# Moving sixteen tokens of the second block from one-hot matmuls to the DRAM gate table

## The chip, the cores and the metric

The kernel runs on one core of a Trainium2 chip. The metric is the device time of one execution in microseconds (us). TensorE is called PE here, VectorE DVE, ScalarE ACT, GpSimd POOL and SyncE SP, as in the profile. A name with a q (SPq, ACTq) is an engine's queue at work on a DMA issue.

## The reference

A two-layer decoder block on 256 tokens is followed by a second block that ends in a PEER layer, and the change touches only that layer. Each of 8 heads selects 16 of 128 x 128 experts for each token, and the gates are a softmax over the 16 scores:

```python
best, pos = lax.top_k(cand.reshape(T, PEER_HEADS, PEER_TOPK * PEER_TOPK), PEER_TOPK)
experts = jnp.take_along_axis(cand_idx..., pos, axis=-1)
gates = jax.nn.softmax(best, axis=-1).astype(h.dtype)
...
act = jax.nn.gelu(jnp.einsum('cd,ced->ce', xb, ub), approximate=False) * gb
return jnp.einsum('ce,ced->cd', act, vb)
```

## The kernel before

The kernel doesn't gather experts. It computes gelu(u_e . x) for all 16384 experts and 256 tokens, multiplies by a dense table of gates that is zero where an expert was not chosen, and multiplies the result by all v_e. `big` is [128 i, 128 j, 256 tokens] in SBUF.

The back part has four stages. In the **pq stage** p_q and p_s compute the scores. In the **u stage** (the loop over `c`, two keys each, 128 keys) PE runs 24 matmuls for a key (`proj_stat`, mm3 at L329 to L331). Between keys, `pump` hands out the routing of the tokens in pieces (`RU`): the top-16 searches on DVE, token block 0 first and block 1 after it. Every piece has a price in credits, and each key brings 1.3 credits. In the **hot stage**, the keys from HOT0 on in the same loop, block 1's gates are made by one-hot matmuls: `hot_make` builds one-hot tiles for four tokens on DVE, `hot_mm` runs four 128x128 matmuls on PE (L1581), and the result multiplies `big`. There is one such group of four tokens a key, 32 groups for 128 tokens. `gelu` treats the columns that already have gates apart, in the single buffer `gx`, and the product L1596 runs on DVE for up to 48 columns a key and on POOL above that. In the **v stage** `big` goes through `asplit` into the last product.

Block 0's 128 tokens take another way. Their gates are scattered into a zeroed table `gd` in DRAM by POOL's indirect DMAs with add (`scatter`, one for each head and rank, 128 in all, L1492, each preceded by a small memset). A head's DMAs are declared independent of each other; the next head's wait for them. The table is read back two keys at a time (`g_load`) and multiplied in on POOL (`g_mul`, L1539).

Weights come through `Stream`: SP loads 1 MB, ACT makes the rounded half `wh` (L231) and DVE the rest `wl` (L243). In the back part wh and wl have three buffers each, and the two halves of a key are written into the program two keys ahead of its matmuls, so wh of key n+3 may start when PE has finished key n.

Each engine works through its own instructions in program order, so one that waits holds up those behind it on that engine. A DMA issue is an instruction of the engine that issues it.

Of the kernel before, what the change touches and what calls it, by code (L numbers as in the profile page):

```python
# [9 lines left out]
F32 = mybir.dt.float32  # L10
I32 = mybir.dt.int32
# [4 lines left out]
OP = mybir.AluOpType  # L16
# [11 lines left out]
LAM_INIT = 0.8 - 0.6 * math.exp(-0.3 * 0)  # L28
NEG = -1.0e30
NE = 128  # L30
NZ = 32
CRED0, CRED1 = 2.0, 1.3
HOT0 = 91


def stat_pack(w):
# [227 lines left out]
def body(ctx, tc, I, O):  # L264
    nc = tc.nc
    V, A, P, G = nc.vector, nc.scalar, nc.tensor, nc.gpsimd
# [5 lines left out]
    dp = ctx.enter_context(tc.tile_pool(name="dp", bufs=1, space=bass.MemoryType.DRAM))  # L272
# [576 lines left out]
    lctx.close()  # L849

    fp2 = f2ctx.enter_context(tc.tile_pool(name="fp2", bufs=2))
    gd = dp.tile([128 * NE * 128, 1], F32, name="gd")
    gz = gd.rearrange("(a p f) o -> a p (f o)", a=NZ, p=128)
    zt = fp2.tile([128, 256], F32, name="zt", bufs=1)
    V.memset(zt, 0.0)
# [608 lines left out]

    spacer = bx.tile([1, 1], F32, name="spacer", bufs=1)

    BATCH = [(0, 1), (1, 3), (3, 5), (5, 8)]

    def weights(t, a, b):
        g, v = gate[:, t, a:b, :], best[:, t, a:b, :]  # L1470
        V.tensor_tensor(g, v, v[:, :, 0:1].to_broadcast([128, b - a, 16]), op=OP.subtract)
        A.activation(g, g, AF.Exp)

    def address(a, b):
        v = best[:, 0, a:b, :]
        V.scalar_tensor_tensor(v, ei[:, 0, a:b, :], float(NE), ej[:, 0, a:b, :], op0=OP.mult, op1=OP.add)
        V.tensor_scalar(v, v, 128.0, tok[:, 0:1], op0=OP.mult, op1=OP.add)
        V.tensor_copy(idx[:, a:b, :], v)

    def normal(t, a, b):  # L1480
        g = gate[:, t, a:b, :]
        su = bx.tile([128, 8], F32, name="gsu")[:, 0:b - a]
        V.tensor_reduce(su, g, axis=AX.X, op=OP.add)
        V.reciprocal(su, su)
        V.tensor_tensor(g, g, su[:, :, None].to_broadcast([128, b - a, 16]), op=OP.mult)

    sent = []

    def scatter(h):
        for k in range(16):  # L1490
            G.memset(spacer, 0.0)  # L1491
            d = G.indirect_dma_start(  # L1492
                out=gd, out_offset=bass.IndirectOffsetOnAxis(ap=idx[:, h, k:k + 1], axis=0),
                in_=gate[:, 0, h, k:k + 1], in_offset=None, compute_op=OP.add)
            for oh, o in sent:
                if oh == h:
                    tc.declare_no_dep(d.ins, o.ins, reason="other experts of one head")
            sent.append((h, d))

    def batch(a, b):  # L1500
        def first():
            weights(0, a, b)
            address(a, b)

        def second():
            normal(0, a, b)
            for h in range(a, b):
                scatter(h)

        return [(0.5, first), (0.4, second)]  # L1510

# [9 lines left out]
                    RU.extend(batch(a, b))  # L1521
    for i in range(8):
        RU.extend(route(i, 1))
    RU.extend([(0.5, lambda: weights(1, 0, 8)), (0.6, lambda: normal(1, 0, 8))])

    W.sub = [V, V]
    gv = gd.rearrange("(i j t) o -> i j (t o)", j=NE, t=128)
    GT = {}

    def g_load(c):  # L1530
        if c == 0:
            GT["t"] = bx.tile([128, 4, 2, 128], F32, name="oj", bufs=1)
        GT[c] = GT["t"][:, c % 4]
        nc.sync.dma_start(GT[c], gv[:, 2 * c:2 * c + 2, :])

    def g_mul(c):
        if c < NE // 2:
            b = big[:, 2 * c:2 * c + 2, 0:128]
            G.tensor_tensor(b, b, GT.pop(c), op=OP.mult)  # L1539

    for c in range(NE // 2):
# [46 lines left out]
    def gelu(c, ps):  # L1588
        n = 4 * HB[0]
        p3 = ps.rearrange("p (a b) -> p a b", a=2)  # L1590
        b = big[:, 2 * c:2 * c + 2, :]
        A.activation(b[:, :, :S - n], p3[:, :, :S - n], AF.Gelu)
        if n:
            x = bx.tile([128, 2, 128], F32, name="gx", bufs=1)
            A.activation(x[:, :, :n], p3[:, :, S - n:], AF.Gelu)
            late.append(lambda: (V if n <= 48 else G).tensor_tensor(b[:, :, S - n:], b[:, :, S - n:], x[:, :, :n], op=OP.mult))  # L1596

# [6 lines left out]
    for c in range(NC):  # L1604
        w = W.get(("u", c))
        ps = bank()
        if 2 * c + 2 >= NE - 32:
            assert not RU
        for k in range(2):
            e = 2 * c + k - HOT0  # L1610
            if 1 <= e < 33:
                hot_make(e - 1)
            w(k)
            while pend:
                pend.pop(0)()
            if c == NC - 1 and k == 1:
                g_mul(0)
                as0 = bx.tile([128, 4, 256], F32R, name="oi", bufs=1)
                AV += [(as0[:, 0, :], as0[:, 1, :]), (as0[:, 2, :], as0[:, 3, :])]
                asplit(0)  # L1620
                asplit(1)
            proj_stat(ps[:, k * 256:k * 256 + 256], w, k, xT)
            pump(CRED1)
            if e >= 0:
                assert not RU
            if e == 0:
                hot_T()
            gated()
            if 2 <= e < 34:
                hot_mm(e - 2, 2 * c)  # L1630
        pend.append(lambda c=c, ps=ps: gelu(c, ps))
    pend.pop(0)()
# [78 lines left out]
```

## Time and profile before

| what | value |
|---|---|
| time, median of 3 runs (lowest, highest) | 1691.44 us (1689.56, 1692.04) |
| the profiled execution | 1689.98 us, its span 1688.2 us |
| PE busy | 1644.9 us, 97% of the span |
| DVE, ACT, POOL busy | 1172.8, 814.9, 478.5 us (69%, 48%, 28%) |
| mean granted clock of PE | 0.993 |

A span is what the profile covers, and the 1.78 us between it and the execution's own time lie outside. Busy shares are means over stages, so the argument reads one stage at a time. A row of a timeline gives start, duration, engine, line, operation, tiles, and in square brackets how long the engine had been idle and whose event ended that.

### The profile page before, as it was taken

Reading aid. Unit: us, or ns where it says so; the run is one execution under the profiler, and the core shown is the slowest. Engines: PE = TensorE matmul, PEld = TensorE weight load, DVE = VectorE, ACT = ScalarE, POOL = GpSimd, SP = SyncE. Lnnn points to the kernel's source line nnn. Section 1 sums busy time; section 2 is a strip of 40 time slices with the busy share of each in tenths; the row PEclk is TensorE's granted clock in tenths of the full one; section 3 lists DMA queues with packets and bytes.
Section 4 is the critical chain, followed back from the end, with each engine's and each line's share of the span. In section 5 each row is a group of like instructions: output and inputs, shape, how many; then the busy total and the mean of one; then the engine's idle time right before and its main releaser. Section 6 shows DMA issues by size and latency. Waiting matters only on the chain.

```text
span 1688.2 us, 27583 instructions
## 1 busy us (share of the span) xinstructions
PE 1644.9 (97%) x11013; PEld 1499.3 (89%) x11013; DVE 1172.8 (69%) x2069; ACT 814.9 (48%) x1260; POOL 478.5 (28%) x446
## 2 busy tenths in 40 slices
PE   8899999999999998999999999999999999999997
PEld 6888999899999986897889999999999888888886
DVE  5897554666655465876557898899899666666665
ACT  5564444444444444564454555444433544444444
POOL 0542000110300012302025788878701211111111
PEclk9999999999999999999999999999999999999999
DMA  7436877455555545424445666766634666666665
GB/s 274 143 134 237 262 237 249 175 198 189 204 197 178 197 175 187 152 98 162 138 152 178 181 190 176 198 178 185 164 131 147 200 221 202 219 207 214 212 209 175
DMA packets 80417, 317.48 MB, mean 188 GB/s; under 512 B 25121, under 2 KB 41761, under 8 KB 45345
## 3 DMA queue, kind: packets, MB, share of 16 engines
q1 hardware_dynamic: 59120, 304.38, 52.5%
q0 software_dynamic: 20736, 10.56, 4.2%
q8 instruction: 86, 1.41, 0.3%
q10 hardware_dynamic: 432, 0.79, 0.1%
q14 instruction: 43, 0.34, 0.1%
HBM read 303.04 MB, written 10.55 MB: 186 GB/s over the span
## 4 chain that ended last, share of the span: by engine, by line
PE 55%; DVE 3%; issue 1%; DMA 1%; ACT 1%; POOL 1%; POOLq 0%; DVEq 0%; ACTq 0%; SPq 0%
PE mm L329 9%; PE mm L331 9%; PE mm L330 9%; PE acc L330 8%; PE acc L329 8%; PE acc L331 7%; PE acc L1581 2%; DMA xTl<-mTl 1%; DVE qkm L1062 1%; POOL wl L243 0%; PE mm L1460 0%; PE mm L1336 0%; PE mm L1303 0%; DVE wl L243 0%; DVE r L453 0%
## 5 line engine op out<-in xcount | busy, mean ns | idle before, releaser
L243 DVE TENSOR_TENSOR wl<-raw,wh 128x1024 fp32r<-128x1024 f32 (+1 forms) x511 | 630.8, 1253 | 259.4 <-ACT wh L231 257.6
L231 ACT ACTIVATE wh<-raw 128x1024 fp32r<-128x1024 f32 (+1 forms) x537 | 553.6, 1055 | 376.1 <-PE acc L331 186.8
L329 PE MATMUL mm<-xTh,wh 128*128 128x256 f32 x2328 | 659.3, 283 | 1.2 <-DVE mTl L378 1.1
L331 PE MATMUL mm<-xTh,wl 128*128 128x256 f32 x2328 | 654.9, 281 | 2.4 <-DVE wl L243 2.0
L330 PE MATMUL mm<-xTl,wh 128*128 128x256 f32 x2328 | 654.2, 281 | 0.0
L329 PEld LDWEIGHTS mm<-xTh,wh 128*128 128x128 f32 x2328 | 440.8, 189 | 4.0 <-DVE mTl L378 1.5
L331 PEld LDWEIGHTS mm<-xTh,wl 128*128 128x128 f32 x2328 | 440.4, 189 | 3.3 <-DVE wl L243 2.4
L330 PEld LDWEIGHTS mm<-xTl,wh 128*128 128x128 f32 x2328 | 440.8, 189 | 0.9
L1492 POOL DMA_INDIRECT gd<-slots,idx x128 | 253.0, 1977 | 68.9 <-issue 32.0
L330 PE MATMUL acc<-wl,xTh 128*128 128x512 f32 x632 | 251.7, 398 | 0.1
L329 PE MATMUL acc<-wh,xTh 128*128 128x512 f32 x632 | 250.6, 397 | 0.0
L243 POOL TENSOR_TENSOR wl<-raw,wh 128x1024 fp32r<-128x1024 f32 x26 | 64.7, 2494 | 565.1 <-ACT wh L231 563.3
L331 PE MATMUL acc<-wh,xTh 128*128 128x512 f32 x504 | 197.6, 392 | 0.0
L329 PEld LDWEIGHTS acc<-wh,xTh 128*128 128x128 f32 x632 | 119.1, 188 | 30.4 <-issue 0.7
L330 PEld LDWEIGHTS acc<-wl,xTh 128*128 128x128 f32 x632 | 119.0, 188 | 27.2 <-DVE wl L243 0.6
L1539 POOL TENSOR_TENSOR big<-big,oj 128x256 f32<-128x256 f32 x64 | 56.8, 888 | 289.8 <-DMA oj<-gd 289.8
L331 PEld LDWEIGHTS acc<-wh,xTh 128*128 128x128 f32 x504 | 94.6, 188 | 22.8
L880 DVE TENSOR_TENSOR sil<-sil,mm 128x256 f32<-128x256 f32 x44 | 18.5, 421 | 105.5 <-ACT sil L879 105.5
L879 ACT ACTIVATE sil<-mm 128x256 f32<-128x256 f32 x44 | 16.9, 385 | 151.2 <-PE mm L331 151.2
L362 DVE TENSOR_TENSOR xTh<-big,xTh 128x256 fp32r<-128x256 f32 x126 | 80.5, 639 | 0.0
L1491 POOL MEMSET spacer<- 1x1 f32 x128 | 78.6, 614 | 0.0
L330 PE MATMUL acc<-wl,hTh 128*128 128x512 f32 x176 | 69.6, 395 | 0.0
(388 smaller groups left out, 1838.4 us busy)
## 6 DMA issues: line engine op xcount, KB each, us to landing
raw<-in_ws_dram SPq DMA_DIRECT2D x131, 1024.0 KB
raw<-in_us_dram SPq DMA_DIRECT2D x64, 1024.0 KB
raw<-in_vs_dram SPq DMA_DIRECT2D x64, 1024.0 KB
gd<-zt SPq DMA_DIRECT2D x32, 256.0 KB
raw<-in_pq_dram SPq DMA_DIRECT2D x8, 1024.0 KB
oj<-gd SPq DMA_DIRECT2D x64, 128.0 KB
gb<-in_vec_dram POOLq DMA_DIRECT2D x12, 512.0 KB
gd<-slots,idx POOLq DMA_INDIRECT x128
```

The lines of the kernel that those rows point to most:

```text
L231: self.nc.scalar.activation(h[:, s], self.R[i][:, k * HW:(k + 1) * HW][:, s], AF.Copy)
L243: self.sub[k].tensor_tensor(l[:, s], self.R[i][:, k * HW:(k + 1) * HW][:, s], h.bitcast(F32)[:, s], op=OP.subtract)
L329: P.matmul(ps, lh, rh, start=first, stop=False)
L330: P.matmul(ps, lh, rl, start=False, stop=False)
L331: P.matmul(ps, ll, rh, start=False, stop=last)
L362: V.tensor_tensor(l, src, h.bitcast(F32), op=OP.subtract)
L879: A.activation(s, pg[:, :256], AF.Silu)
L880: V.tensor_tensor(s, s, pg[:, 256:], op=OP.mult)
L1491: G.memset(spacer, 0.0)
L1492: d = G.indirect_dma_start(out=gd, out_offset=bass.IndirectOffsetOnAxis(ap=idx[:, h, k:k + 1], axis=0), in_=gate[:, 0, h, k:k + 1], in_off ...
L1539: G.tensor_tensor(b, b, GT.pop(c), op=OP.mult)
L1581: P.matmul(ps[:, i * 128:i * 128 + 128], oi[:, i, :], oj[:, i, :], start=True, stop=True)
```

## The change

The table gets rows for 144 tokens instead of 128 (`TT`), so block 1's first sixteen tokens use it too, and the one-hot way keeps 112 (NG = 28 groups; HOT0 moves from key 91 to 95). A scatter wants 128 partitions: the sixteen tokens' 16 ranks are spread over them into `pack` by small DMAs on ACT's queue, eight strips of two ranks for the addresses and eight for the gates. A cast on DVE makes integer addresses `idx1` from `pack`, and each head then needs two scatters instead of sixteen. Block 1's softmax is cut into three batches of heads (0 to 1, 2 to 4, 5 to 7), each with its own strips and cast. The scatters of block 0's heads 5 to 7 now stand behind the first two of these batches, each together with a head of block 1.

```diff
-NZ = 32
+NZ = 36
+TT = 144
-HOT0 = 91
+HOT0 = 95
+NG = (2 * 128 - TT) // 4
...
-    gd = dp.tile([128 * NE * 128, 1], F32, name="gd")
+    gd = dp.tile([128 * NE * TT, 1], F32, name="gd")
...
+    pack = bx.tile([128, 2, 8, 2], F32, name="pack", bufs=1)
+    idx1 = bx.tile([128, 8, 2], I32, name="idx1", bufs=1)
+    groups = [((0, 5), (1, 0)), ((0, 6), (1, 1)), ((0, 7), (1, 2))] + [((1, h),) for h in range(3, 8)]
+    def batch1(a, b):
+        def first():
+            weights(1, a, b)
+            address(1, a, b)
+        def second():
+            normal(1, a, b)
+            for q in range(8):
+                for i, src in enumerate((best, gate)):
+                    A.dma_start(pack[16 * q:16 * q + 16, i, a:b, :], src[0:16, 1, a:b, 2 * q:2 * q + 2])
+            V.tensor_copy(idx1[:, a:b, :], pack[:, 0, a:b, :])
+            while groups and groups[0][-1][1] < b:
+                scatter(*groups.pop(0))
+        return [(0.7, first), (0.7, second)]
...
-            for h in range(a, b):
-                scatter(h)
+            for h in range(a, min(b, 5)):
+                scatter((0, h))
...
-    RU.extend([(0.5, lambda: weights(1, 0, 8)), (0.6, lambda: normal(1, 0, 8))])
+        for a, b in BATCH1:
+            if b == i + 1:
+                RU.extend(batch1(a, b))
...
-            GT["t"] = bx.tile([128, 4, 2, 128], F32, name="oj", bufs=1)
-        GT[c] = GT["t"][:, c % 4]
+            GT["t"] = bx.tile([128, 1024], F32, name="oj", bufs=1)
+        a = c % 3 * 2 * TT
...
-            if 1 <= e < 33:
+            if 1 <= e < NG + 1:
                 hot_make(e - 1)
```

On DVE, right behind the routing of block 1's second head (`big<-big,tf` and the sum into `slots` end it), the program before went on with the next head's search (MAX):

```order
L1428 TENSOR_TENSOR big<-cst,af 128x256
L1430 TENSOR_TENSOR big<-big,tf_11422 128x256
L1431 TENSOR_REDUCE slots<-big 128x16
L243 TENSOR_TENSOR wl<-raw,wh 128x1024
L1387 MAX tv_11592<-big 128x8
```

After the change the first batch of block 1 stands there:

```order
L1433 TENSOR_REDUCE slots<-big 128x16
L245 TENSOR_TENSOR wl<-raw,wh 128x1024
L1474 TENSOR_TENSOR slots<-slots 128x32
L1479 SCALAR_TENSOR_TENSOR slots<-slots 128x32
L1480 TENSOR_SCALAR slots<-slots,cst 128x32
L1487 TENSOR_REDUCE gsu<-slots 128x2
L1488 RECIPROCAL gsu<-gsu 128x2
L1489 TENSOR_TENSOR slots<-slots,gsu 128x32
L1518 CAST idx_8825<-pack 128x4
L245 TENSOR_TENSOR wl<-raw,wh 128x1024
```

Seven instructions moved between two wl, and the last of them, the cast (idx_8825 is `idx1`), reads what ACT's DMAs bring.

On ACT, at the same place of the program, before:

```order
L1592 ACTIVATE big<-mm 128x512
L231 ACTIVATE wh<-raw 128x1024 x2
L1592 ACTIVATE big<-mm 128x512
```

and now:

```order
L1619 ACTIVATE big<-mm 128x512
L1475 ACT_TABLE_LOAD
L1475 ACTIVATE slots<-slots 128x32
L1517 DMA pack<-slots 16x2x2 x16
L233 ACTIVATE wh<-raw 128x1024 x2
L1619 ACT_TABLE_LOAD
L1619 ACTIVATE big<-mm 128x512
```

Two table loads, one exponential and sixteen DMA issues stand between a gelu (L1592, now L1619) and the next wh. The batches of three heads look the same with 16x3x2; in the last one a wl stands behind the address (TENSOR_SCALAR) and a wh ahead of the DMAs.

On POOL, the last scatters ahead of the gelu products (now L1623), before:

```order
L1491 MEMSET spacer 1x1
L1492 DMA gd<-slots,idx 2097152x1
L1596 TENSOR_TENSOR big<-big,gx 128x2x52
L1596 TENSOR_TENSOR big<-big,gx 128x2x60
```

and now:

```order
L1496 MEMSET spacer 1x1
L1497 DMA gd<-pack,idx_8825 2359296x1
L1623 TENSOR_TENSOR big<-big,gx 128x2x52
L1623 TENSOR_TENSOR big<-big,gx 128x2x60
```

POOL's queue holds 144 scatters instead of 128 ahead of these products, and the last ten belong to five heads of block 1 with two each.

## Rows read from the trace of the kernel before

**Rows 1.** The page's busy time of each engine.

```profile
PE 1644.9 (97%) x11013; PEld 1499.3 (89%) x11013; DVE 1172.8 (69%) x2069; ACT 814.9 (48%) x1260; POOL 478.5 (28%) x446
```

**Rows 2.** Busy time by stretch: two windows of the u and v stages.

```profile
core 0: us, PE busy (x) PEld busy (x) DVE busy (x) ACT busy (x) POOL busy (x), PEclk, DMA share, GB/s
...
1100.00:1150.00 50.00, 50.00 (x423) 50.00 (x423) 44.96 (x118) 23.13 (x27) 39.82 (x40) 1.00 0.68 190
...
1340.00:1500.00 160.00, 160.00 (x688) 128.71 (x687) 101.88 (x116) 77.85 (x114) 24.88 (x29) 1.00 0.62 212
```

**Rows 3.** The chain that ended last, pq, u and hot stages: start, us, what.

```profile
927.02 1.84 PE mm L1460 x16
1190.89 0.33 PE mm L1563 x3
1196.91 0.89 PE acc L1581 x8
1200.62 0.89 PE acc L1581 x8
```

**Rows 4.** Timeline of ACT, u stage.

```profile
1076.88 1.06 ACT L231 ACTIVATE wh<-raw 128x1024 fp32r<-128x1024 f32 x1 [1.79 <-PE mm L330]
...
1079.73 1.06 ACT L231 ACTIVATE wh<-raw 128x1024 fp32r<-128x1024 f32 x1 [1.30 <-PE mm L330]
```

**Rows 5.** Timeline of DVE, the same place.

```profile
1077.98 1.22 DVE L243 TENSOR_TENSOR wl<-raw,wh 128x1024 fp32r<-128x1024 f32 x1 [0.38 <-ACT wh L231]
1079.12 0.29 DVE L1387 MAX8 tv<-big 128x8 f32<-128x128 f32 x1
```

**Rows 6.** Timeline of DVE: ends of a three-head batch of block 0.

```profile
1040.50 0.20 DVE L1471 TENSOR_TENSOR slots<-slots 128x48 f32<-128x48 f32 x1
...
1041.95 1.23 DVE L243 TENSOR_TENSOR wl<-raw,wh 128x1024 fp32r<-128x1024 f32 x1
```

**Rows 7.** Timeline of ACT: a table load, and a DMA issue with its successor.

```profile
1043.84 1.28 ACT L1592 ACT_TABLE_LOAD   x1
...
1682.48 0.37 ACTq L1685 DMA_DIRECT2D out_dram<-big  x1
1682.90 0.72 ACT L1682 ACTIVATE big<-big,rs 128x512 f32<-128x512 f32 x1 [0.45 <-POOL rs L320]
```

**Rows 8.** Timeline of SP: DMA issues that follow one another.

```profile
0.73 1.34 SPq L213 DMA_DIRECT2D raw<-in_ws_dram  x3
16.27 0.98 SPq L579 DMA_DIRECT2D cst<-in_cst_dram  x2
```

**Rows 9.** Timeline of POOL: first scatters of heads 0, 4, 5, 6, and the end.

```profile
908.81 2.38 POOL L1492 DMA_INDIRECT gd<-slots,idx  x1 [14.01 <-DVE slots L1485]
1071.05 1.56 POOL L1492 DMA_INDIRECT gd<-slots,idx  x1 [3.74 <-DMA gd<-slots,idx]
1110.88 1.56 POOL L1492 DMA_INDIRECT gd<-slots,idx  x1 [4.35 <-DVE big L1428]
1151.16 1.56 POOL L1492 DMA_INDIRECT gd<-slots,idx  x1 [2.13 <-DMA gd<-slots,idx]
1219.79 1.56 POOL L1492 DMA_INDIRECT gd<-slots,idx  x1 [0.27 <-issue]
1244.77 1.17 POOL L1596 TENSOR_TENSOR big<-big,gx 128x104 f32<-128x104 f32 x1 [23.42 <-ACT gx L1595]
```

**Rows 10.** Busy time by stretch: an idle time of PE and what followed.

```profile
659.00:664.00 5.00, 0.59 (x3) 0.34 (x2) 0.00 (x0) 0.99 (x3) 0.00 (x0) 0.79 0.98 402
664.00:669.00 5.00, 5.00 (x13) 3.90 (x13) 2.36 (x2) 3.88 (x5) 0.00 (x0) 0.53 0.15 30
```

**Rows 11.** PE's waits: us in total, times, longest.

```profile
PE mm L329 <- ACT vs L1002: 4.4, 1, 4.4
```

**Rows 12.** Timeline of POOL, v stage: one product with the table.

```profile
1359.55 0.97 POOL L1539 TENSOR_TENSOR big<-big,oj 128x256 f32<-128x256 f32 x1 [4.63 <-DMA oj<-gd]
```

**Rows 13.** Timeline of ACT, v stage: the split that reads it.

```profile
1361.37 0.40 ACT L361 ACTIVATE xTh<-big 128x256 fp32r<-128x256 f32 x1
```

More of the change, by code (lines that the diff above doesn't have):

```diff
@@ L1465, in body @@
     spacer = bx.tile([1, 1], F32, name="spacer", bufs=1)
+    BATCH1 = [(0, 2), (2, 5), (5, 8)]
     BATCH = [(0, 1), (1, 3), (3, 5), (5, 8)]
@@ L1472, in weights, with address @@
         A.activation(g, g, AF.Exp)
[L1474 to L1478, printed above, removed]
+    def address(t, a, b):
+        v = best[:, t, a:b, :]
+        V.scalar_tensor_tensor(v, ei[:, t, a:b, :], float(NE), ej[:, t, a:b, :], op0=OP.mult, op1=OP.add)
+        V.tensor_scalar(v, v, float(TT), tok[:, t:t + 1], op0=OP.mult, op1=OP.add)
+        if t == 0:
+            V.tensor_copy(idx[:, a:b, :], v)
     def normal(t, a, b):
@@ L1485, in normal, with scatter @@
         V.tensor_tensor(g, g, su[:, :, None].to_broadcast([128, b - a, 16]), op=OP.mult)
[L1487 to L1498, printed above, removed]
+    def scatter(*heads):
+        group = []
+        for t, h in heads:
+            ix, g = ((idx, gate[:, 0]), (idx1, pack[:, 1]))[t]
+            for k in range((16, 2)[t]):
+                G.memset(spacer, 0.0)
+                d = G.indirect_dma_start(
+                    out=gd, out_offset=bass.IndirectOffsetOnAxis(ap=ix[:, h, k:k + 1], axis=0),
+                    in_=g[:, h, k:k + 1], in_offset=None, compute_op=OP.add)
+                for o in group:
+                    tc.declare_no_dep(d.ins, o.ins, reason="other tokens, or other experts of one head")
+                group.append(d)
+    pack = bx.tile([128, 2, 8, 2], F32, name="pack", bufs=1)
[14 more added lines that the diff above has]
+        return [(0.7, first), (0.7, second)]
     def batch(a, b):
@@ L1502, in first @@
             weights(0, a, b)
-            address(a, b)
+            address(0, a, b)
         def second():
             normal(0, a, b)
-            for h in range(a, b):
-                scatter(h)
+            for h in range(a, min(b, 5)):
+                scatter((0, h))
         return [(0.5, first), (0.4, second)]
@@ L1523, in body @@
         RU.extend(route(i, 1))
-    RU.extend([(0.5, lambda: weights(1, 0, 8)), (0.6, lambda: normal(1, 0, 8))])
+        for a, b in BATCH1:
+            if b == i + 1:
+                RU.extend(batch1(a, b))
     W.sub = [V, V]
-    gv = gd.rearrange("(i j t) o -> i j (t o)", j=NE, t=128)
+    gv = gd.rearrange("(i j t) o -> i j (t o)", j=NE, t=TT)
     GT = {}
@@ L1531, in g_load @@
         if c == 0:
-            GT["t"] = bx.tile([128, 4, 2, 128], F32, name="oj", bufs=1)
-        GT[c] = GT["t"][:, c % 4]
+            GT["t"] = bx.tile([128, 1024], F32, name="oj", bufs=1)
+        a = c % 3 * 2 * TT
+        GT[c] = GT["t"][:, a:a + 2 * TT].rearrange("p (j t) -> p j t", j=2)
         nc.sync.dma_start(GT[c], gv[:, 2 * c:2 * c + 2, :])
@@ L1537, in g_mul @@
         if c < NE // 2:
-            b = big[:, 2 * c:2 * c + 2, 0:128]
+            b = big[:, 2 * c:2 * c + 2, 0:TT]
             G.tensor_tensor(b, b, GT.pop(c), op=OP.mult)
@@ L1593, in gelu @@
         if n:
-            x = bx.tile([128, 2, 128], F32, name="gx", bufs=1)
+            x = bx.tile([128, 2, 4 * NG], F32, name="gx", bufs=1)
             A.activation(x[:, :, :n], p3[:, :, S - n:], AF.Gelu)
@@ L1606, in body @@
         ps = bank()
-        if 2 * c + 2 >= NE - 32:
-            assert not RU
+        if 2 * c + 1 >= HOT0:
+            assert not RU and not groups
         for k in range(2):
             e = 2 * c + k - HOT0
-            if 1 <= e < 33:
+            if 1 <= e < NG + 1:
                 hot_make(e - 1)
@@ L1628, in body @@
             gated()
-            if 2 <= e < 34:
+            if 2 <= e < NG + 2:
                 hot_mm(e - 2, 2 * c)
```

## The prediction, made before the run

> **What bounds the kernel now.** I read the busy times first: PE is busy for 97% of the span [rows 1]. A mean hides stages, so the windows come next: in the u stage PE is busy for all of 50 us, in the v stage for all of 160 us, at granted clock 1.00 [rows 2]. DVE is the next engine, with 44.96 of 50 us. So in the stages that the change touches two things move the end: PE work that goes away, and any wait that PE doesn't have now. The chain of work that ended last gives PE's pace. From the end of the last p_s matmul (927.02 + 1.84 = 928.86) to the transposes of hot_T at 1190.89 there are 92 keys, 2.85 us each [rows 3]. In the hot stage the groups of one-hot matmuls follow each other at 3.71 us [rows 3], so a group costs PE 0.86 us.
>
> How much can PE's suppliers be late? Stream lets wh of a key start when PE has finished the key three before it. The wh that starts at 1076.88 was released by PE [rows 4]; counted from 928.86 at 2.85 us, 52 keys (0 to 51) had ended, so it belongs to key 54. PE comes to key 54 two keys later, at 1076.88 + 5.70 = 1082.6, and needs wl with its third matmul, 0.24 us on, at 1082.8. DVE has that wl done at 1077.98 + 1.22 = 1079.20 [rows 5]. The lead is 3.6 us, and three buffers allow no more: DVE had itself waited 0.38 us for wh [rows 5]. This is the number against which every new wait on DVE or ACT is held.
>
> **The change part by part.**
>
> *Removed.* Four groups of one-hot matmuls, 4 x 0.86 = 3.4 us of PE. PE is never idle in this stage, so all of it is on the path: -3.4 us. The four groups' work on DVE and ACT lies beside PE and gives nothing more.
>
> *Moved.* HOT0 is four keys later because the batches have more pieces in the queue of credits. The keys themselves cost the same.
>
> *The batches of block 1.* Before, block 1's softmax was one piece with no DMA. Now there are three batches, each a chain across DVE, ACT, the DMA queues and DVE again, and the cast that ends it stands in DVE's queue ahead of the next wl. Behind the cast wait wl, and behind wl PE. I follow the first batch, which stands behind wl of key 54 as counted above; T is the end of that wl, 1079.20.
>
> - The six small DVE instructions. Block 0's batch of three heads took 1041.95 - 1040.50 = 1.45 us with one cast more [rows 6]; I take 1.4. The exponential's table load of 1.28 us [rows 7] can run while ACT has nothing else, since ACT waits 1.3 to 1.8 us for PE at each key [rows 4].
> - The DMA issues. Addresses and gates alternate; the second DMA needs the gates, so from there ACT issues one after another, and the cast needs the fifteenth, the last of the addresses. Three issues on SP took 1.34 us and two took 0.98 [rows 8], 0.45 to 0.49 each from start to start. On ACT one takes 0.37 us, and the next activation starts behind it [rows 7]. I take 0.46, as back-to-back issues are the nearest row: 13 x 0.46 = 6.0 us to the start of the fifteenth, and 0.4 for itself. The ends are 0.37 and 0.49.
> - The landing. The nearest rows are also of scattered 4-byte elements: the first scatter of a head waits for the landing of the last one of the head before, 2.13 us at one place and 3.74 at another [rows 9]. I take 2.2, because nothing accumulates here, and keep 3.7 as the upper end.
> - The cast, 0.2 us, and the next wl, 1.2 us.
>
> Together 1.4 + 6.0 + 0.4 + 2.2 + 0.2 + 1.2 = 11.4 us from T. PE wants that wl one key after the one before, at T + 3.6 + 2.85 = T + 6.45. So PE waits 4.9 us. The second batch is the same, 4.9. In the third a wl stands behind the first three small instructions, which leaves 0.8 us less in the chain: 4.1. The sum is 13.9 us of PE waiting. Lower end: 13 x 0.37 + 0.4 + 2.1 + 2.8 = 10.1, so 3.7, 3.7 and 2.9, or 10.3. Upper end: 13 x 0.49 + 0.5 + 3.7 + 2.8 = 13.4, so 6.9, 6.9 and 6.1, or 19.9.
>
> The Trainium skill speaks against this order of work (DMA: Bandwidth & Descriptors, Rules for kernel authors): it advises to issue a DMA early, compute, and wait for its semaphore late. The cast waits at once. The same page (Issuing engines are not separate DMA queues) also says that the time in which a sequencer starts a DMA is usually small beside the DMA itself. Here the rows say the opposite, 6.4 us of issuing to 2.2 of landing; an estimate by that sentence, with no time for the issues, makes the chain 5 us, which the lead would cover.
>
> *What a stall does to PE's clock.* After an idle time of 4.4 us [rows 11] the granted clock was 0.79 over the 5 us that hold the wait and 0.53 over the next 5 [rows 10]. In these 5 us PE was busy throughout, and 0.47 of 5.0, 2.35 us, were lost. A wait of 4 to 5 us in the u stage is that long, but follows a full PE; no row shows such a one. Bounds are 0 and 2.35 each; I take 2.0, nearer to the row, and 6 us for three. The level would be the lower of the two, 1.2 GHz for a time.
>
> *POOL's scatters.* A head takes (1110.88 - 908.81) / 5 = 40.4 us with its wait [rows 9], 2.4 a scatter, so POOL is the pacer of the table and not routing. Heads 5 to 7 with two more scatters each take some 45 us apiece at that pace, and less late in the stage (heads 6 and 7 together took 70.2 us, from 1151.16 to 1221.35, against 80.8 at the mean pace): from 1110.88 to about 1241. Then five heads with two each, 3.9 us and a landing of 2.2: to about 1272. Before, the end was at 1221.4, and the first gelu product on POOL at 1244.77 [rows 9], 23 us of slack. That product comes four keys of 2.85 us later, at 1256, and with the three stalls (20 us with the clock) at 1276. So the stalls hide POOL's tail. Without them it would be late; that is a rival below.
>
> *Edits at nothing.* Four more zero fills of 256 KB lie in the first feed-forward stage, far ahead of their reader. The table's reads and products grow by an eighth: 0.97 us becomes 1.1, and ACT's split starts 0.85 us after the product's end (1361.37 against 1360.52) [rows 12, 13], which covers 0.1 for the product and 0.1 for the load; without that cover 64 x 0.2 us could at most be lost. Three slots for four in the table's buffer: each is free again when POOL's product has run, and a product takes a fifth of its 5.6 us. Four more table loads of 1.28 us on ACT lie inside ACT's idle time or the stalls.
>
> Sum: -3.4 + 13.9 + 6.0 = +16.5 us on the profiled execution's own 1689.98, or 1706.5. The median of the runs is 1.46 us above that execution, so I say 1707.
>
> **The rivals.**
>
> 1. *The stalls without the clock.* For it: the u stage keeps PE full up to the wait, and the row on the clock is from a stage with gaps. Time: 1689.98 + 10.5 = 1700.5.
> 2. *The lead covers the chain.* This is the other side: if issues are so quick that the chain stays under 6.45 us, no PE wait appears and the four groups are pure gain, 1689.98 - 3.4 = 1686.6. It decides at an issue spacing of (6.45 - 1.4 - 0.4 - 2.2 - 1.4) / 13 = 0.08 us. Against it stands every row of rows 7 and 8. It is also what would follow from the skill's sentence on small issue times.
> 3. *Covered, but POOL's tail comes late.* As 2, but POOL gets to its first gelu product at 1272 instead of 1256. The next gelu, 7.4 us after the first, can't write `gx`, ACT stands until 1273.4 instead of 1263.6, and wh and wl behind it come 9.8 us late against a lead of about 4: PE waits 6 us. -3.4 + 6 = +2.6, or 1692.6.
> 4. *Longer chains.* The small DMAs share the queues with 1 MB loads (DMA share 0.68 in the u stage [rows 2]) and with the scatters; at the upper end of issue and landing, with the clock's 7 us, +23.5, or 1713.5, and beyond if a DMA must wait for a load that is in flight.
>
> **How the numbers follow.** Forecast 0.50, rival 1 0.24, rival 4 0.12, rival 3 0.05, rival 2 0.06, and 0.03 that the parts cancel to nothing. Within 0.2%, 3.4 us, is about what a measurement of this kernel can't tell from no change. Faster gets rival 2, 0.06; same gets rival 3 and the cancelling, 0.08; slower the rest, 0.86. The range holds the forecast, rival 1 and most of rival 4, and takes in the bounds: the low end -3.4 + 10.3 = +6.9 gives 1697, and I start at 1696; the upper end 1713.5 plus the median's 1.5 gives 1715.
>
> **What would show it.** In the changed profile: three idle times of PE of 4 to 5 us near 1085, 1145 and 1210, ended by DVE's wl; DVE's cast waiting 7 to 8 us for a DMA on `pack`; sixteen ACT issues 0.46 us apart; PE's granted clock below 1 behind each wait; 28 groups at 3.71 us; POOL's scatters ending near 1272 with no wait of ACT for POOL behind it. The prediction is wrong if the cast finds its data there, if PE has no idle time in the u stage, or if the v stage has gaps from late table reads.

## The result, and the profile after

| kernel | median | ratio to before |
|---|---|---|
| before | 1690.86 us (1689.56 to 1692.04) | |
| after | 1715.85 us (1713.73 to 1717.52) | 1.0146 [1.0133, 1.0159] |

The change makes the kernel slower by 1.46%, 25 us, where the forecast was 16 us slower and its upper end 1715. The profiled execution of after took 1717.52 us, its span is 1715.7 us and its mean granted clock 0.986. The answer to [rows 1] is the page's busy time of each engine:

```profile
PE 1651.3 (96%) x10981; PEld 1504.7 (88%) x10981; DVE 1173.3 (68%) x2062; ACT 820.5 (48%) x1260; POOL 508.3 (30%) x476
```

The totals say almost nothing, and PE's busy time has even grown by 6.4 us although 32 matmul records are gone, eight for each of the four groups. The waits of PE between 1000 and 1330 us, that is in the u stage and the hot stage, say more. The columns are the total, the number of times and the longest; before, this list is empty for the same stretch.

```profile
engine line waited for: us in total, times, longest us
PE mm L331 <- ACT wh L233: 18.6, 3, 6.3
PE mm L333 <- DVE wl L245: 1.8, 3, 0.7
```

PE waits 20.4 us, and it is not DVE's wl but ACT's wh that ends 18.6 of them. The windows show the first idle stretch and what follows each of the three (the other two are 6.14 and 6.16 us long, at 1153.58 and 1222.75), and two rows that answer to [rows 2]:

```profile
core 0: us, PE busy (x) PEld busy (x) DVE busy (x) ACT busy (x) POOL busy (x), PEclk, DMA share, GB/s
1086.67:1092.94 6.27, 0.01 (x1) 0.01 (x1) 0.00 (x0) 1.12 (x2) 5.46 (x8) 0.70 0.25 1
1092.94:1099.45 6.51, 5.91 (x26) 5.62 (x27) 6.24 (x22) 3.71 (x4) 5.70 (x8) 0.50 0.62 163
1099.45:1106.00 6.55, 6.55 (x57) 6.55 (x57) 4.96 (x10) 3.29 (x4) 5.74 (x6) 1.00 0.66 163
...
1159.72:1164.30 4.58, 3.86 (x16) 3.56 (x17) 4.22 (x12) 3.71 (x4) 3.98 (x5) 0.50 0.65 125
...
1228.91:1235.98 7.07, 6.61 (x29) 6.32 (x30) 5.44 (x9) 5.53 (x7) 6.26 (x7) 0.50 0.41 85
1100.00:1150.00 50.00, 50.00 (x424) 50.00 (x423) 44.09 (x114) 23.97 (x28) 40.64 (x40) 1.00 0.70 190
1340.00:1500.00 160.00, 160.00 (x724) 130.44 (x723) 103.33 (x114) 79.19 (x118) 28.69 (x32) 1.00 0.62 212
```

In the idle stretch PE is busy for 0.01 us. When it resumes, the granted clock is 0.50, the lower level (1.2 GHz), for 6.5, 4.6 and 7.1 us, and then 1.00 again. PE is busy for 5.91 + 3.86 + 6.61 = 16.4 us at half clock; half of that, 8.2 us, is what these stretches cost. The lower clock alone is less: a matmul follows the next at 0.214 us there and at 2.85 / 24 = 0.119 later, which for the 71 matmuls (26 + 16 + 29) makes 6.7 us. Most of the rest lies in the first matmuls behind each wait, which start 0.38 us apart. Between the stalls, and in the v stage, PE is as full as it was in [rows 2].

ACT at the first stall shows what held wh (the line with x16 groups the sixteen regrouping DMAs of one batch):

```profile
1080.90 0.23 ACT L1475 ACTIVATE slots<-slots 128x32 f32<-128x32 f32 x1
1081.31 10.40 ACTq L1517 DMA_DIRECT2D pack<-slots  x16
1091.82 2.00 ACT L233 ACTIVATE wh<-raw 128x1024 fp32r<-128x1024 f32 x2 [10.69 <-DMA pack<-slots]
...
1100.61 1.06 ACT L233 ACTIVATE wh<-raw 128x1024 fp32r<-128x1024 f32 x1 [3.92 <-DMA raw<-in_us_dram]
```

And DVE at the same place; the answer to [rows 5] is its first line.

```profile
1079.14 1.22 DVE L245 TENSOR_TENSOR wl<-raw,wh 128x1024 fp32r<-128x1024 f32 x1 [0.38 <-ACT wh L233]
...
1081.59 0.19 DVE L1489 TENSOR_TENSOR slots<-slots,gsu 128x32 f32<-128x32 f32 x1
1092.94 0.17 DVE L1518 CAST idx<-pack 128x4 int32<-128x4 f32 x1 [11.16 <-DMA pack<-slots]
1093.04 1.23 DVE L245 TENSOR_TENSOR wl<-raw,wh 128x1024 fp32r<-128x1024 f32 x1
```

Both queues that feed PE stand still for over 10 us: ACT issues from 1081.31 to 1091.71, and wh follows; DVE waits 11.16 us with the cast, and wl follows. The releaser that the profile names in ACT's 10.69 is only the DMA that landed last; ACT waited for its own issues. The chain that ended last, at the same place, gives the price of each step (three of the issues that it goes through are shown, and one matmul at half clock):

```profile
1081.59 0.20 DVE slots L1489
...
1082.09 0.60 ACTq L1517
1082.72 0.61 ACTq L1517
...
1089.83 0.60 ACTq L1517
...
1090.47 2.39 DMA pack<-slots
...
1092.94 0.06 DVE idx L1518
...
1093.04 1.24 DVE wl L245
...
1094.90 0.21 PE mm L331
```

From the second issue to the fifteenth it is 1090.47 - 1082.09 = 8.38 us, 13 x 0.645. The fifteenth has landed 2.4 us after its start. Over all 48 the view of the tile `pack` has (duration in ns, lowest, median, highest):

```profile
L1517 ACTq DMA_DIRECT2D pack<-slots x48: 592/605/946, 1081.3 to 1227.1; - x48
```

The sum, by rows. The stage begins with the end of the last p_s matmul, 927.02 + 1.84 before [rows 3] and 928.17 + 1.85 = 930.02 after; from there to the end of the span it is 759.3 us before and 785.7 after, +26.4. Of these, -3.4 are the four groups, +18.6 + 1.8 the waits, +8.2 the half clock with the first matmuls behind the waits, and 0.9 the hot stage, where the 28 groups follow at (1339.39 - 1238.46) / 27 = 3.74 us in place of 3.71 [rows 3]. That makes 26.1. The 0.9 can't be put down to the change: run 2 below, with the same three stalls, and version 10 run the same 28 groups at 3.71, and the pace of the same instructions differs a little between executions (last section). The first and the last of these rows:

```profile
1238.46 0.89 PE acc L1608 x8
...
1339.39 0.89 PE acc L1608 x8
```

The remaining 1.15 us of the span lie ahead of the stage, where the change does nothing but zero fills; such shifts appear between all the kernels below (927.2 to 929.6 for the start of this row), so nothing is made of it. POOL's end answers to the last two of [rows 9]:

```profile
1268.70 1.60 POOL L1497 DMA_INDIRECT gd<-pack,idx  x1 [0.27 <-issue]
1286.67 1.17 POOL L1623 TENSOR_TENSOR big<-big,gx 128x104 f32<-128x104 f32 x1 [16.37 <-ACT gx L1622]
```

### The profile page after: what moved, and what is told of

Read it like the earlier page. It is cut to its first block, busy times and chain, and to the rows that moved or that the text cites. A ratio compares the mean times of both kernels' runs of the same rounds, so it can differ in the third digit from the quotient of the medians.

```text
span 1715.7 us, 27603 instructions
## 1 busy us (share of the span) xinstructions
PE 1651.3 (96%) x10981; PEld 1504.7 (88%) x10981; DVE 1173.3 (68%) x2062; ACT 820.5 (48%) x1260; POOL 508.3 (30%) x476
## 4 chain that ended last, share of the span: by engine, by line
PE 53%; DVE 3%; issue 2%; ACTq 2%; ACT 1%; DMA 1%; POOL 1%; POOLq 0%; DVEq 0%
PE mm L333 9%; PE mm L331 9%; PE mm L332 9%; PE acc L333 8%; PE acc L332 7%; PE acc L331 7%; ACTq L1517 2%; PE acc L1608 1%; DMA xTl<-mTl 1%; DVE wl L245 1%; DVE qkm L1064 1%; ACT wh L233 0%; POOL wl L245 0%; PE mm L1462 0%; PE mm L1338 0%
## 5 line engine op out<-in xcount | busy, mean ns | idle before, releaser
L331 PE MATMUL mm<-xTh,wh 128*128 128x256 f32 x2328 | 663.4, 285 | 19.7 <-ACT wh L233 18.6
L1566 POOL TENSOR_TENSOR big<-big,oj 128x288 f32<-128x288 f32 x64 | 59.6, 931 | 287.2 <-DMA oj<-gd 287.2
L1496 POOL MEMSET spacer<- 1x1 f32 x144 | 88.8, 617 | 0.0
L364 DVE TENSOR_TENSOR xTh<-big,xTh 128x256 fp32r<-128x256 f32 x126 | 85.5, 678 | 0.0
```

The costliest lines, as they stand in the source:

```text
L331: P.matmul(ps, lh, rh, start=first, stop=False)
L364: V.tensor_tensor(l, src, h.bitcast(F32), op=OP.subtract)
```

## The experiments

The theory after this reading (A): the loss is the sixteen DMA issues in ACT's queue, together with the cast that waits on DVE, three times over, and PE's lower clock behind each of the three waits. The rivals: only the cast and the landing hold PE (B), the larger table and the added scatters carry the loss (C), the clock costs nothing. Unless a diff says otherwise it is against after. Each ratio is to runs of before on the same chip.

**1. No regrouping DMAs.** Scatters of the sixteen tokens go to fixed cells that no token uses.

```diff
+    V.tensor_scalar(own, iota[:, 0:16], 1.0, 128.0, op0=OP.mult, op1=OP.add)
+    V.scalar_tensor_tensor(own, tok[:, 0:1].to_broadcast([128, 16]), float(NE * TT), own, op0=OP.mult, op1=OP.add)
+    V.tensor_copy(idx1.rearrange("p a b -> p (a b)"), own)
...
-            for q in range(8):
-                for i, src in enumerate((best, gate)):
-                    A.dma_start(pack[16 * q:16 * q + 16, i, a:b, :], src[0:16, 1, a:b, 2 * q:2 * q + 2])
-            V.tensor_copy(idx1[:, a:b, :], pack[:, 0, a:b, :])
```

> The 48 regrouping DMAs and the cast behind them are left out; the sixteen tokens' scatters go to fixed cells with a gate of zero, so their gates are left out of the result. Theory A (the loss is the sixteen DMA issues in ACT's queue and the cast that waits on DVE, three times, and PE's half clock after each): no PE idle time near 1087, 1154 and 1223, granted clock 1.00 there, the gain of four one-hot groups stays, 1687 to 1688 us; if POOL's scatters, which still end near 1269, are now late for the first gelu product on POOL, one PE wait of about 6 us near 1265 and 1692 to 1693. Rival C (the larger table, the ten more scatters or the longer table reads cost the time): still above 1705.

Measured: 1691.34 us, ratio 0.9994 [0.9985, 1.0004]. PE's only wait from 1000 us on is 0.4 us, and the clock stays at 1.00. All of the 25 us are gone with the 48 DMAs and the cast, so C falls. POOL's tail is there, as rival 3 of the prediction had it, first on POOL and then on ACT:

```profile
1270.98 0.99 POOL L1624 TENSOR_TENSOR big<-big,gx 128x104 f32<-128x104 f32 x1
```

```profile
1272.01 0.27 ACT L1623 ACTIVATE gx<-mm 128x120 f32<-128x120 f32 x1 [6.82 <-POOL big L1624]
...
1272.28 1.06 ACT L233 ACTIVATE wh<-raw 128x1024 fp32r<-128x1024 f32 x1
```

ACT stands 6.82 us for `gx`, but the wh behind it is only 4.9 us late (due about 3.7 us after the one of 1263.75, at 1267.4), and the lead takes all but 0.4 us of it. Rival 3's mechanism is real, its price was 0.4 us and not 6. In the profiled execution the stage's time (from the end of the last p_s matmul, 928.91 + 1.84, to 1687.1) is 756.4 us, 3.0 less than before: the four groups less this 0.4. The timed runs show less of it, -0.5 us at the median, with an interval from -2.5 to +0.7.

**2. Issues alone.** The fixed indices of 1, with the DMAs kept and only the cast gone, so DVE never waits for a DMA.

```diff
-            V.tensor_copy(idx1[:, a:b, :], pack[:, 0, a:b, :])
```

> The 48 DMAs are issued as they are, but the indices come from a fixed table and DVE's cast, which waited for them, is gone (the sixteen tokens' gates land in fixed cells). Theory A1 (ACT is blocked by its own issues: wh of the next key stands behind sixteen issues of 0.65 us): PE still idles three times, by about 5 us each instead of 6.2, since the landing and the cast drop out but wh and then wl must still follow the last issue; the clock still falls; 1709 to 1715 us. Rival B (what holds PE is only DVE's cast and the landing, as the prediction's chain has it, so that ACT's wh would have been in time): no PE idle time, 1687 to 1693 us.

Measured: 1715.47 us, ratio 1.0140 [1.0123, 1.0157], as slow as after. PE's waits:

```profile
PE mm L331 <- ACT wh L233: 18.6, 3, 6.2
PE mm L333 <- DVE wl L245: 1.4, 3, 0.5
```

ACT's own issues are enough to explain the whole loss, and B falls in the form in which it clears ACT. Waits of about 5 us were expected; that they are as long as in after says that the landing and the cast added nothing to them there.

**3. Issues on SP.** The other half: ACT is free, DVE's cast waits as in after.

```diff
-                    A.dma_start(pack[16 * q:16 * q + 16, i, a:b, :], src[0:16, 1, a:b, 2 * q:2 * q + 2])
+                    nc.sync.dma_start(pack[16 * q:16 * q + 16, i, a:b, :], src[0:16, 1, a:b, 2 * q:2 * q + 2])
```

> After's kernel with the 48 regrouping DMAs issued from SP instead of ACT; DVE's cast still waits for them at once. ACT's wh is then free. Theory A (ACT's queue and DVE's cast are each enough to hold PE): chain 1.4 + 14 x 0.645 + 0.6 + 1.7 + 0.2 + 1.2 = 14.1 us against 6.45, so three waits of 7 to 8 us ended by wl instead of wh, the clock falls as before, 1714 to 1722 us. Rival (ACT's blocked queue alone is the loss, and SP, whose issues of large loads are 0.33 to 0.49 us, is quick): waits under 4 us, 1703 us or less.

Measured: 1716.60 us, ratio 1.0154 [1.0139, 1.0170]. PE's waits, and one batch in SP's queue:

```profile
PE mm L333 <- DVE wl L245: 21.2, 3, 7.5
```

```profile
1077.68 0.33 SPq L217 DMA_DIRECT2D raw<-in_us_dram  x1
1081.49 10.30 SPq L1517 DMA_DIRECT2D pack<-slots  x16
```

Two more things could have held PE here, and didn't: SP's next 1 MB load starts only at 1094.03, but ACT's wh ran on time ahead of it (1081.18, 1083.93), and wl started at 1092.78, right behind the cast. On SP the sixteen issues take the same 10.3 us, so 0.64 us belongs to this DMA and not to ACT, and the 1 MB load beside it takes 0.33. The path that the prediction followed is also enough by itself. In after the two run side by side, and taking away either leaves the other.

**4. One pair for a batch.** The cast still waits, but for one pair of DMAs (the fixed indices of 1 serve for the other experts).

```diff
-            for q in range(8):
+            for q in range(1):
...
-            V.tensor_copy(idx1[:, a:b, :], pack[:, 0, a:b, :])
+            V.tensor_copy(idx1[0:16, a:b, :], pack[0:16, 0, a:b, :])
```

> One pair of DMAs for a batch instead of eight pairs, and the cast still waits for them (the sixteen tokens keep two of their sixteen experts; the others go to fixed cells with gate zero). Chain from the end of a wl: 1.5 small instructions + 1.3 for two issues + 2.0 landing + 0.2 cast + 1.2 wl = 6.2 us against a budget of 6.45. Theory A: no PE wait or less than 0.7 us each, the clock stays at 1.00, 1687 to 1694 us with POOL's tail as in the run without DMAs. Rival B (the landing and the waiting cast are the larger part): waits of 2 us or more remain, above 1698 us.

Measured: 1691.96 us, ratio 0.9998 [0.9986, 1.0009]; PE waits 0.5 us once. The first batch on DVE:

```profile
1084.58 0.19 DVE L1489 TENSOR_TENSOR slots<-slots,gsu 128x32 f32<-128x32 f32 x1
1086.50 0.16 DVE L1523 CAST idx<-pack 16x4 int32<-16x4 f32 x1 [1.73 <-DMA pack<-slots]
```

A landing that DVE waits for at once costs nothing as long as the chain stays inside the budget of 6.45 us. The number of issues is what breaks it. The four groups' gain doesn't show in the median. In the profiled execution (1692.77 us) the reason is PE's pace: a key took 2.88 us in place of 2.85 (last section), 3 us over the u stage. The other executions, from 1687.33 to 1695.30 us, left no trace.

**5. One batch of eight heads.** As many DMAs as one batch of after, with four times the bytes of its first.

```diff
-    BATCH1 = [(0, 2), (2, 5), (5, 8)]
+    BATCH1 = [(0, 8)]
-    groups = [((0, 5), (1, 0)), ((0, 6), (1, 1)), ((0, 7), (1, 2))] + [((1, h),) for h in range(3, 8)]
+    groups = [((1, h),) for h in range(8)]
...
-            for h in range(a, min(b, 5)):
+            for h in range(a, b):
```

> After's kernel with all eight heads of the sixteen tokens in one batch behind the last routing piece: sixteen DMAs once instead of three times, each of 16 partitions x 8 heads, and POOL's scatters of block 0 no longer paired. Theory A (each batch costs one wait of about 6.2 us plus about 3 us of half clock, independent of how many heads it carries): one PE idle time of 6 to 7 us near 1200 to 1210, one fall of the clock, 6.5 + 3 - 3.4 = +6 us on before, 1697 to 1699 us. Rival (the wait goes with the bytes, so a batch of eight heads waits as long as the three together): 18 us of idle time, 1710 us or more.

Measured: 1697.18 us, ratio 1.0039 [1.0027, 1.0051]. PE waits for wh once, 6.3 us, and twice for wl, 0.8 us together; an issue takes 0.61 us at the median, as in after. Four times the bytes cost the same: the price goes with the number of DMAs.

**6. PE kept busy.** Ahead of each of the three late keys (`FILL` counts three keys from the batch) PE gets matmuls that nobody reads, so that it doesn't idle.

```diff
+            while FILL and FILL[0] == 0:
+                FILL.pop(0)
+                zz = accp.tile([128, 512], F32, name="acc11")
+                for n in range(56):
+                    P.matmul(zz[:, 0:256], xT[0][:, n % KT, 0:128], xT[0][:, n % KT, :], start=True, stop=True)
             proj_stat(ps[:, k * 256:k * 256 + 256], w, k, xT)
```

> After's kernel with 56 matmuls of 128x256 whose result nobody reads, placed on PE just ahead of each of the three keys that wait, so that PE is busy for about 6.2 us of each wait. Theory D (about 9 of the 27 us are PE at its lower clock behind the three idle times): granted clock 1.00 throughout the u stage, the waits themselves stay filled, so 1706 to 1708 us, some 9 us less than after. Rival (the clock's fall costs nothing, the loss is all in waits): 1714 to 1718 us.

Measured: 1710.60 us, ratio 1.0114 [1.0098, 1.0131], 18.8 us above before where after is 25.0 above. The windows over the three places:

```profile
1085.00:1100.00 15.00, 13.76 (x111) 13.18 (x110) 7.95 (x23) 6.82 (x8) 12.88 (x15) 1.00 0.48 76
1150.00:1166.00 16.00, 15.07 (x125) 14.66 (x124) 8.69 (x25) 7.33 (x8) 13.85 (x17) 1.00 0.57 120
1218.00:1236.00 18.00, 17.58 (x149) 17.37 (x148) 10.98 (x22) 8.42 (x12) 12.62 (x16) 1.00 0.42 88
```

The clock stays at 1.00, and 6.2 us come back, not 9; the intervals of the two ratios leave this uncertain by some 3 us. The traces are sharper. By the starts of the keys, the four, two and three keys at the three places took 21.3, 14.7 and 19.7 us in after and 20.1, 13.8 and 17.1 here, 4.7 us less; the rest of the 7.3 us by which the stage is shorter in this profiled execution is PE's pace at the other keys (last section). The filling is dearer than the waits that it covers: 3 x 56 matmuls at 0.119 us are 20.0 us, and 2.5 us of waits remain, together 2.1 more than the 20.4 of after. So the full clock gives back 4.7 + 2.1 = 6.8 us, close to the 6.7 that the spacing of the matmuls said. The idle time is the cause of the lower clock.

**7. The table alone.** This one is an edit of the kernel before: the larger table, its fills and its slots, with no regrouping.

```diff
-NZ = 32
+NZ = 36
+TT = 144
...
-            GT["t"] = bx.tile([128, 4, 2, 128], F32, name="oj", bufs=1)
-        GT[c] = GT["t"][:, c % 4]
+            GT["t"] = bx.tile([128, 1024], F32, name="oj", bufs=1)
+        a = c % 3 * 2 * TT
+        GT[c] = GT["t"][:, a:a + 2 * TT].rearrange("p (j t) -> p j t", j=2)
```

> The kernel before with the larger table alone: 36 zero fills, cells of 144, three slots of 144 columns for the reads, and nothing of the regrouping (the products still take 128 columns, and all 32 one-hot groups stay). The prediction's edits at nothing: within 0.1% of before, 1689 to 1692 us, no PE wait in the last feed-forward stage. Rival (the table's longer reads, its slots or the fills carry part of the loss): 1.5 us or more above before.

Measured: 1690.44 us, ratio 1.0000 [0.9991, 1.0009], and no wait of PE from 1000 us on. The edits at nothing cost nothing.

**8. Strips in one run of bytes.** DVE turns the rows first; a DMA then carries addresses and gates together, in one contiguous run for each partition.

```diff
-            for q in range(8):
-                for i, src in enumerate((best, gate)):
-                    A.dma_start(pack[16 * q:16 * q + 16, i, a:b, :], src[0:16, 1, a:b, 2 * q:2 * q + 2])
+            for i, src in enumerate((best, gate)):
+                V.tensor_copy(turn[0:16, :, i, :, :], src[0:16, 1, a:b, :].rearrange("p h (q k) -> p q h k", q=8))
+            for q in range(8):
+                A.dma_start(pack[16 * q:16 * q + 16, 4 * a:4 * b], turn[0:16, q].rearrange("p i h k -> p (i h k)"))
```

> After's kernel, but DVE first turns the sixteen tokens' rows (two copies of some 0.2 us), so that a strip carries addresses and gates together and has one contiguous run of 32 or 48 bytes in each of its 16 partitions: eight DMAs for a batch instead of sixteen, SBUF to SBUF and on ACT as before, and the cast waits at once. What makes an issue of 0.60 us, where the regrouping through DRAM took 0.33? View E (the strided form of a strip with its three dimensions): issues fall to about 0.33, 0.37 apart; chain 1.4 + 0.5 + 7 x 0.37 + 2.0 + 0.2 + 1.2 = 7.9 us against 6.45, PE waits 1.5 us three times, 1691 to 1696 us. View F (SBUF to SBUF over 16 partitions, whatever the form): issues stay at 0.6, 0.645 apart; chain 9.8 us, PE waits 3.4 us three times and the clock falls in part, 1699 to 1708 us.

Measured: 1699.12 us, ratio 1.0044 [1.0028, 1.0059]. The issues, and PE's waits:

```profile
L1525 ACTq DMA_DIRECT2D pack<-gx x24: 514/611/905, 1081.0 to 1211.8; - x24
```

```profile
PE mm L331 <- ACT wh L233: 5.2, 3, 1.8
PE mm L333 <- DVE wl L245: 3.0, 3, 1.2
```

View F: the form of the strip is not what makes an issue 0.6 us. With half as many issues the waits are 8.2 us in place of 20.4, and the clock still falls three times.

**9. Through DRAM, and late.** Two DMAs for a batch in place of sixteen: one writes the turned rows to DRAM in the target's order, one reads them back to 128 partitions. They stand in pieces of their own between the routing pieces of the next head, the cast and the scatters in a third one.

```diff
+            for i, src in enumerate((best, gate)):
+                V.tensor_copy(turn[0:16, :, i, :, :], src[0:16, 1, a:b, :].rearrange("p h (q k) -> p q h k", q=8))
+            A.dma_start(hop[:, :, 4 * a:4 * b].rearrange("q p x -> p q x"), turn[0:16].rearrange("p q i h k -> p q (i h k)"))
+
+        def third():
+            A.dma_start(pack[:, 4 * a:4 * b], hop.rearrange("q p x -> (q p) x")[:, 4 * a:4 * b])
+
+        def fourth():
+            V.tensor_copy(idx1[:, a:b, :], mine[:, 0])
...
-HOT0 = 95
+HOT0 = 97
...
-(V if n <= 48 else G)
+(V if n <= 64 else G)
```

> A version that should beat both: DVE turns the sixteen tokens' rows to the order of the target (two small copies), one DMA writes them to DRAM and one reads them back to 128 partitions a key or more later, and the cast and the scatters come later still, so ACT issues 2 DMAs for a batch instead of 16 and nothing waits at once. hot_T two keys later, and the products of the first 16 groups on DVE so that POOL's tail is hidden. Theory A: no PE wait near 1087, 1154 and 1223, clock 1.00, the four groups are gained: 3.4 us under before, 1686 to 1689 us. Rival (the detour through DRAM or the reads behind it hold ACT or DVE again): waits of PE of 2 us or more in these places, 1692 us or more.

Measured: 1689.48 us, ratio 0.9988 [0.9979, 0.9997], and one wait of PE, at another place:

```profile
PE acc L331 <- ACT oi L363: 1.5, 1, 1.5
```

It stands ahead of the first v matmul. The table's first read can't start before the last one-hot group has left the buffer, and the groups now end with the last but one key.

**10. The same, one key earlier.** `HOT0 = 96`, nothing else.

> The version with the regrouping through DRAM, and hot_T one key earlier than there (one key later than in after), because its only PE wait of 1.5 us, ahead of the first matmul of the v stage, came from the table's first read behind the last one-hot group. Theory A: no PE wait from 1000 us on, 3 to 3.5 us under before, ratio 0.998. Rival (the wait stays, another read holds it): as that version, 1.5 to 2 us under before.

Measured: 1685.41 us, ratio 0.9966 [0.9955, 0.9978]. No wait of PE from 1000 us on. Its two kinds of DMAs and the cast, with the first and the last start:

```profile
L1528 ACTq DMA_DIRECT2D pack<-hop x3: 326/326/345, 1083.9 to 1203.3; - x3
L1531 DVE CAST idx<-pack x3: 163/163/217, 1097.5 to 1206.0; 128x6 int32<-128x6 f32 x2, 128x4 int32<-128x4 f32 x1
...
L1525 ACTq DMA_DIRECT2D hop<-gx x3: 325/326/334, 1082.1 to 1199.3; - x3
```

This version beats both kernels. In the profiled execution the stage takes 1685.8 - (928.23 + 1.84) = 755.7 us, 3.6 less than before: the four groups, by their working 3.4. The timed runs gain 5.8 us at this ratio.

**11 and 12. Where the rest of the gain is not.** Version 10 with the products' limit back at 48, and the kernel before with that limit at 64.

```diff
-(V if n <= 64 else G)
+(V if n <= 48 else G)
```

> The version through DRAM with hot_T at key 96, but the products of the late columns go to POOL after 12 groups again, as in after, instead of 16. It asks whether POOL's tail costs anything, and whether that version's gain of 6 us, where four groups are worth 3.4, holds on another chip. POOL's scatters end near 1270, ACT waits 5 to 7 us for gx once, PE at most 0.5 us. Expected 0 to 0.5 us above that version, ratio to before 0.997 to 0.998. Rival (the shift of two products to DVE is worth 2 us or more): ratio 0.998 to 0.9995 here, and a gain in the kernel before with the same shift.

> The kernel before with that one edit: the products of the late columns go to POOL after 16 groups instead of 12. PE waits for nothing there in before, so nothing should change: ratio 0.999 to 1.001, 1690 to 1692 us. Rival (it carries part of the 6 us gained): 2 us or more under before.

Measured: 1685.61 us, 0.9965 [0.9952, 0.9977], and 1691.96 us, 1.0001 [0.9992, 1.0010]. The gain holds on another chip, and the limit has no part in it. POOL's scatters again end at 1271.4 us, but the wait of ACT for `gx` that was expected isn't there: with hot_T a key later the next gelu, at 1272.08, finds POOL's product ended at 1271.85. In the profiled execution the stage is 3.5 us shorter than before. That the timed runs gain some 2 us beyond the four groups stays unexplained: no stage of the profiled executions shows it. PE's pace, which differs between executions (last section), could be part of it; that was not tested, as the other executions left no trace.

## Why the prediction was wrong

- **What bounds the kernel, and the budget.** Right. wl of key 54 ends at 1080.36, and PE would have taken up the next one at 1086.74, 6.4 us later (6.45 predicted). Run 4 shows that a chain inside this budget is free, runs 2 and 3 that one beyond it is not.
- **The step that failed: the issues, "I take 0.46".** One issue took 0.605 us and followed at 0.645; thirteen of them were 8.4 us and not 6.0. The chain from the end of that wl was 13.9 us (1080.36 to 1094.28) in place of 11.4, and all of the difference is in this term and in 0.3 us more for the first issue. The rows chosen [rows 7, 8] were of DMAs between DRAM and SBUF with 0.37 to 0.49 us, and the upper end, 0.49, came from them too. The trace of before had dearer ones, which the prediction passed over: SP's 32 zero fills of the table, 0.52 us at the median and 1.18 for two (rows below this list). By the prediction's own reckoning that is 0.59 an issue, 13 x 0.59 = 7.7 us against the 8.4 measured. An SBUF-to-SBUF strip on ACT or SP had no row there. Waits of 7.5 us for that wl follow, where 4.9 were said: 6.3 ended by wh, 0.6 by wl, and the matmuls between them at half clock.
- **The path that was left out.** The prediction let only the cast hold PE. wh of the next key stands in ACT's queue behind all sixteen issues, and run 2 shows that this alone makes the full loss. With 0.46 us an issue it would have been late too (16 x 0.46 + 1.06 for wh), so the omission hardly changed the sum, but a remedy on DVE alone would have brought nothing.
- **The landing.** 2.4 us from the issue's start to the release, against 0.4 + 2.2. Right.
- **The third batch.** Its shorter chain was not shorter in effect: ACT's issues began at 1215.25 for the addresses and went on when the gates were there, behind one more wl, and PE waited 6.2 us for wh.
- **The clock.** The mechanism is right. Read as the prediction read its row, half of PE's busy time at 0.50, it is 2.96, 1.93 and 3.31 us, 8.2 us against 6.0; by the spacing of the matmuls and by run 6 the lower clock itself is 6.7 to 6.8 us, near the forecast. The bound of 2.35 was too low for two of the three: in [rows 10] the clock was back within the 5 us, here only 4.6 to 7.1 us behind the wait. Rival 1, stalls without the clock, falls, and so does rival 2, which needed 0.08 us an issue.
- **The four groups.** -3.4 us: versions 10 and 11 show 3.6 and 3.5 in the stage, run 1 3.0 with its 0.4 of waiting.
- **POOL.** The scatters ended at 1270.3 (1272 said), and the stalls hid them. Rival 3, their price once uncovered, was over-sized: 0.4 us, because the wh that came late was late by 4.9 and not 9.8.
- **Edits at nothing.** Right (run 7). The table load in [rows 7] stands at the gelu's line; the exponential's, 1.28 us at 1079.61 in after, took as long.
- **The sums.** Predicted -3.4 + 13.9 + 6.0 = +16.5; measured -3.4 + 20.4 + 8.2 + 0.9 = +26.1 in the stage. Of the 9.6 between them, 6.5 are the waits, for which the issue spacing, 3 x 2.4 us, is enough; 2.2 are the half-clock stretches, and 0.9 the pace in the hot stage, which isn't the change's. Rival 4 had the direction (longer chains), but by shared queues, and its 1713.5 is near the result by luck: the landing was not longer than said, and in run 3 sixteen issues take 10.3 us in a queue where a 1 MB load takes 0.33, so the chain was long by the issues themselves.

Two rows of the kernel before, for the step that failed; they answer to no group of rows:

```profile
L861 SPq DMA_DIRECT2D gd<-zt x32: 518/519/938, 151.0 to 282.3; - x32
```

```profile
168.19 1.18 SPq L861 DMA_DIRECT2D gd<-zt  x2
```

The Trainium skill (DMA: Bandwidth & Descriptors, Issuing engines are not separate DMA queues) calls the time in which a sequencer starts a DMA usually small beside the DMA. For one strip that is a quarter here, 0.6 of the 2.4 us from the start of its issue to its landing; for sixteen in a row, 10.3 us, it doesn't hold, and the measurement decides. The Trainium skill's advice on the same page (Rules for kernel authors), to issue early and to wait late, agrees with version 10, where the cast stands 13.6 us behind its read in the first batch and 2.7 in the last (1097.5 against 1083.9, 1206.0 against 1203.3) and waits for nothing.

## What to carry to other kernels

Count the DMAs that a change adds to the queue of an engine that also feeds the critical one, price each by a row of the same kind of DMA, or by the dearest row that the trace has where there is none, and hold the sum against the lead of every tile that is produced behind them, on the issuing engine as well as on the one that waits. When the pieces are small, turn them once on a compute engine and move them with few DMAs, even by way of DRAM; and let the instruction that needs the data stand behind other work. A wait of PE of several us was paid twice here: once for itself, and again for the half clock behind it.

## What the runs showed of the hardware

- An issue of a DMA from SBUF to SBUF over 16 partitions took 0.60 us on ACT and 0.59 on SP, with 8-byte pieces (0.605), with one run of 32 or 48 bytes (0.611) and with eight heads (0.612). A write from the same 16 partitions to DRAM, and a read from DRAM to 128 partitions, took 0.326. The pair of memories alone doesn't set the price: the zero fills of before, also from SBUF to DRAM, took 0.52 (rows above). What part the 16 partitions of the target have was not tried.
- The clock fell after much shorter waits as well. In run 8, after 3.93 us in which PE had been busy for 1.12:

```profile
1085.69:1089.62 3.93, 1.12 (x7) 0.90 (x8) 1.95 (x7) 3.38 (x4) 3.39 (x5) 1.00 0.22 1
1089.62:1093.03 3.41, 3.41 (x19) 3.41 (x18) 3.24 (x12) 1.45 (x2) 2.87 (x5) 0.50 0.89 288
```

The single waits of 0.4 us in run 1, 0.5 in run 4 and 1.5 in run 9 left it at 1.00.

- The same instructions at granted clock 1.00, with PE busy throughout, ran at slightly different paces in different executions: between 950 and 1050 us PE has 845 records in before and in after, 835 in run 4 and 855 in run 6. By the starts of PE's first matmul of each key, a key of the u stage took 2.85 us in before and after, 2.88 in run 4 and, up to the first wait, 2.82 in run 6. It changed within an execution too, and in the u stage only at a wait: run 2 had 2.88 us ahead of its first wait and 2.82 behind it (40 us on either side below), run 3 went from 2.85 to 2.82 and back at its first two. That is 1.1% either way, over 1 us in each 100, and over a whole u stage as much as the gain that was sought. What sets it wasn't found.

```profile
1000.00:1040.00 40.00, 40.00 (x335) 40.00 (x334) 35.22 (x92) 17.93 (x22) 33.79 (x33) 1.00 0.68 184
1106.00:1146.00 40.00, 40.00 (x343) 40.00 (x342) 37.72 (x100) 18.25 (x21) 31.68 (x33) 1.00 0.69 186
```
